# First block of a three-block network: table products as one operation for both parts on VectorE, chunk states stored segment-innermost, one recurrence over all groups

## The chip, the core and the metric

The kernel runs on one core of a Trainium2 chip. Its engines are PE (TensorE, matmuls), DVE (VectorE), ACT (ScalarE), POOL (GpSimd) and SP (SyncE, which here only issues DMAs). Each engine works through its own queue in order and waits on semaphores of the others. The metric is the time of one execution in microseconds (us) on the device; lower is better.

## What is computed

The program runs a first block on 512 tokens of width 1024 and then two layers of another network on its result. The change touches the first block alone, and in it the state-space part (S5). Cut to what matters:

```python
h = rms_norm(x, pre_norm_g);  z = h @ w_in
z_q, z_kv, z_kr, g_attn, u_ssm, g_ssm = split(z)
attn = mla_attention(z_q, z_kv, z_kr, ...)          # 4 heads, 512 tokens
attn = rms_norm(attn) * silu(g_attn)
# S5: 32 groups of 16 channels, 64 complex states each, both directions
lam_bar = exp(lam * dt);  b_bar = (lam_bar - 1) / lam * b
h_t = lam_bar * h_(t-1) + b_bar u_t                  # forward, and reversed
y_t = real(C h_t), summed over the directions, + d_skip * u_t
ssm = gelu(y);  ssm = ssm * sigmoid(ssm @ w_glu + b_glu)
ssm = rms_norm(ssm) * silu(g_ssm)
x = x + rms_norm([attn, ssm] @ w_out)
```

## The kernel before

The 128 partitions hold 64 states of the forward direction and 64 of the reversed one. The 512 tokens are 64 chunks of 8. The 32 groups are worked in 8 slices of 4 groups. For each slice there are three steps, and between the first and the second a recurrence:

- `f_slice(s)`: a table of powers of `lam_bar` times `b_bar` (tiles `tb`, `ot`; factors `FP`, `bbr`, `bbi`), transposed on PE (`ftr`, copied by ACT to `f`) and multiplied with the tokens `U` (`vps`). ACT copies the result into the chunk states `st` (L469, L470).
- `recur(hf)`, once for groups 0 to 15 and once for 16 to 31: DVE carries the state over the 64 chunks. `step` is four DVE operations (L488 to L491: tiles `rt`, `rw`). Seven steps run inside segments of 8 chunks, for all 8 segments at once; six steps carry the segment ends; then the corrections `fx` (L510) are added to `st` (L511).
- `prep(s)`: a table of powers times C (factors `EP`, `cc`), written to DRAM (`Ed`, one DMA for each part), and a short convolution kernel from it (`kps` on PE, `kst` on ACT, three small DVE operations), written to DRAM (`Kd`).
- `y_slice(s)`: reads `Ed` back (tile `e`), reads `Kd` as the matrix `T` in 8 DMAs, copies the states to `X` on ACT, and computes `yps` = U T + X e on PE.

A table is complex, so it has a real and an imaginary part, and each part is two products and a sum: three operations of 128x512. In `f_slice` the real part is computed by DVE and the imaginary by POOL; in `prep` both by POOL (L413, L414, L415, called from `half`).

Around this lie the other parts of the block in the order of the program: the two gate projections (`feat`, 8 feature tiles of 24 matmuls each; ACT `th` and `gate`, DVE `gate` L608), the projection of `z_q`, `z_kv`, `z_kr` (`z_tile`), and the attention heads (`head`, scores in tile `sc`), which run in rounds together with the `y_slice` steps. Weights arrive in 512 KB DMAs into a two-buffer stage `wst`; ACT casts them to `whi` (L136) and DVE computes the rest `wlo` (L137); a product is then three matmuls (L167 to L169).

The order in each engine's queue is not the order of the code: the tile framework's scheduler decides it when the program is built. Tiles share slots by tag (`SLOTS1`); a tile waits for its slot's last reader. `E` has 4 slots of 128x512 for the two parts of two tables.

```python
rounds((s, f_slice(s)) for s in range(8))
for hf in range(2): recur(hf)
# gate projections
for s in range(8): prep(s)
# z projection, V, q
rounds([(HEAD0[h], head(h)) for h in range(4)] + [(SL0 + s, y_slice(s)) for s in range(8)])
```

Of the kernel before, what the change touches and what calls it, by code (L numbers as in the profile page):

```python
# [21 lines left out]
SLOTS1 = {"S": 6, "PT": 4, "E": 4, "et": 1, "X": 2, "K": 1, "T": 2, "Y": 1, "sq": 3, "c": 2, "PW": 1, "U": 1, "C": 1, "w": 4}  # L22
# [41 lines left out]
class Net:  # L64
# [116 lines left out]
    def gain(self, name, l, mark=None, tag="PT"):  # L181
        g = [self.act(name="gain", tag=tag) for _ in range(2)]
# [47 lines left out]
    def load_tile(self, src, t, mark=None, tag="S"):  # L230
        x = [self.act(name="x", tag=tag) for _ in range(2)]
# [66 lines left out]
    def block1(self):  # L298
# [3 lines left out]
        G = 32  # L302
# [114 lines left out]
        br, bi = (sm1([128, G, 16], n) for n in ("bbr", "bbi"))  # L417
# [5 lines left out]
        half(bi, nc.gpsimd, wrb, braw[1], wib, braw[0], OP.add, [128, G, 16], "S")  # L423

        EP, FP = sm1([128, 2, 8, G], "EP"), self.act(shape=[128, 2, 8, G], name="FP", tag="S")
        for r in range(2):
            nc.vector.tensor_copy(FP[0:64, r], PW[0:64, r, 1:9][:, ::-1])
            nc.vector.tensor_copy(FP[64:128, r], PW[64:128, r, 1:9])
# [3 lines left out]
        nc.vector.tensor_copy(EP[0:64, 0], PW[0:64, 0, 0:8])  # L432
        nc.vector.tensor_copy(EP[64:128, 0], PW[64:128, 0, 0:8][:, ::-1])
        nc.vector.tensor_scalar(EP[0:64, 1], PW[0:64, 1, 0:8], -1.0, None, OP.mult)
        nc.vector.tensor_scalar(EP[64:128, 1], PW[64:128, 1, 0:8][:, ::-1], -1.0, None, OP.mult)

        def table(P, xr, xi, s, tags, neg, eng):


            sh = [128, 4, 8, 16]  # L440
            gs = slice(s * 4, s * 4 + 4)
            o = [self.act(shape=sh, name="tb", tag=tags[0]) for _ in range(2)]
            pr, pi = (P[:, r, :, gs].rearrange("p e g -> p g e")[:, :, :, None].to_broadcast(sh) for r in range(2))
            xr, xi = (x[:, :, None, :].to_broadcast(sh) for x in (xr, xi))
# [5 lines left out]
        st = self.act(shape=[128, 2, G, 64], name="st", tag="C")  # L450
        nc.vector.memset(st[:, :, :, 0:1], 0.0)

        def f_slice(s):
            gs = slice(s * 4, s * 4 + 4)
            ft = table(FP, br[:, gs], bi[:, gs], s, ("E", "S"), False, nc.vector)
            yield
            f = []
            for r in range(2):
                p = self.ps("sc" if s % 2 else "tr", "ftr")
                for gg in range(4):  # L460
                    nc.tensor.transpose(p[:, gg * 128:(gg + 1) * 128], ft[r][:, gg], self.ident)
# [3 lines left out]
            pv = self.ps("o", "vps").rearrange("p (r g c) -> p r g c", r=2, g=4)  # L465
            for r in range(2):
                for gg in range(4):
                    mm(pv[:, r, gg], f[r][:, gg], U[:, s * 4 + gg], start=True, stop=True)
            nc.scalar.copy(st[0:64, :, gs, 1:64], pv[0:64, :, :, 0:63])  # L469
            nc.scalar.copy(st[64:128, :, gs, 1:64], pv[64:128, :, :, 63:0:-1])  # L470
# [9 lines left out]
        HG = 16  # L480

        def step(gs, dst, src, e, i, n):

            sh = [128, 2, HG, n]
            t, w = (self.small([128, 2, HG, 8], bufs=1, name=x)[:, :, :, :n] for x in ("rt", "rw"))
            ar = PA[:, 0:1, e, gs].to_broadcast([128, 2, HG])[:, :, :, None].to_broadcast(sh)
            ai = PS[:, i, :, gs][:, :, :, None].to_broadcast(sh)
            nc.vector.tensor_tensor(t, ar, st[:, :, gs, src], OP.mult)  # L488
            nc.vector.tensor_tensor(w, ai, st[:, ::-1, gs, src], OP.mult)
# [3 lines left out]
        def recur(hf):  # L493
            gs = slice(hf * HG, hf * HG + HG)
            for j in range(1, 8):
                n = 8 if j < 7 else 7
                step(gs, slice(1 + j, 64, 8), slice(j, 64 if j < 7 else 56, 8), 0, 0, n)
            for q in range(1, 7):
                step(gs, slice(8 * q + 8, 8 * q + 9), slice(8 * q, 8 * q + 1), 7, 1, 1)
            sh = [128, 8, 7, 7]  # L500
            for gh in range(2):
                g8 = slice(hf * HG + gh * 8, hf * HG + gh * 8 + 8)
                for r in range(2):
                    e = nc.vector
                    d = st[:, r, g8, 8:64].rearrange("p g (s j) -> p g s j", j=8)[:, :, :, 1:8]
                    for r2 in range(2):
                        c = st[:, r2, g8, 8:64:8][:, :, :, None].to_broadcast(sh)
                        pw = PA[:, r ^ r2, 0:7, g8].rearrange("p j g -> p g j")[:, :, None, :].to_broadcast(sh)
                        t = self.act(shape=sh, name="fx", tag="S")
                        e.tensor_tensor(t, c, pw, OP.mult)  # L510
                        e.tensor_tensor(d, d, t, OP.subtract if (r, r2) == (0, 1) else OP.add)  # L511
# [7 lines left out]
        Ed = self.dpool.tile([8, 2, 128, 512], F32, name="Ed")  # L519
        Kd = self.dpool.tile([8, 4, 16, 15, 16], F32, name="Kd").rearrange("s g h j x -> s h g (j x)")  # L520

        def prep(s):
# [69 lines left out]
        for hf in range(2):  # L592
            recur(hf)
# [29 lines left out]
        def z_tile(t):  # L623
# [17 lines left out]
            for i in range(2):  # L641
                nc.gpsimd.tensor_tensor(zn[:, 384 + i * 64:448 + i * 64], ka, kb, OP.add)
# [874 lines left out]
```

## Time and profile before

| | us |
|---|---|
| median of 3 runs (1711.34 to 1712.43) | 1712.42 |
| the profiled execution, its own time | 1714.23 |
| span of that execution, first to last instruction | 1712.4 |

| engine | busy us | share of the span |
|---|---|---|
| PE | 1600.2 | 93% |
| DVE | 1026.3 | 60% |
| ACT | 788.3 | 46% |
| POOL | 502.2 | 29% |

The shares are means over a long program of unlike stages. The first block takes the first 400 us or so of the span, and the rest belongs to the two layers behind it. An engine's share says nothing on a stage: each stage is read with the busy times of that stretch alone. Times given as "start" count from the start of the span.

### The profile page before, as it was taken

The page shows a single profiled execution, that of the slowest core. Times are in us where ns is not written, and L with a number is a line of the kernel's source. Part 1 is how long each engine was busy: PE and PEld are TensorE (multiplying, and loading weights), DVE is VectorE, ACT ScalarE, POOL GpSimd, SP SyncE. Part 2 cuts the span into 40 slices and gives each one's busy share as a digit, 9 for nine tenths or more (in the row PEclk, how much of TensorE's full clock was granted, in tenths as well). Part 3 has the DMA queues.
Part 4 walks back from the last instruction along what each step waited for, and adds up shares of the span by engine and source line. Part 5 has one row for each costly group of instructions (what it writes and reads, how often), then busy time and mean ns, then how long its engine had stood idle before and what let it go on. Part 6 is the DMA issues. An engine that isn't in the chain of part 4 may idle for free.

```text
span 1712.4 us, 22709 instructions
## 1 busy us (share of the span) xinstructions
PE 1600.2 (93%) x8240; PEld 1344.7 (79%) x8240; DVE 1026.3 (60%) x2003; ACT 788.3 (46%) x1540; POOL 502.2 (29%) x557
## 2 busy tenths in 40 slices
PE   7776699989999999999999999999999999999998
PEld 5655588778887878888888888787877888888886
DVE  7999955774589886423333346569986632333334
ACT  5432256743467774333232334358774443314142
POOL 3756622240445551201010122135462110101012
PEclk9888899999999999999999999999999999999999
DMA  4122241353410123233333333430123233332332
GB/s 154 50 68 69 77 133 50 99 195 114 155 32 27 51 80 124 93 99 99 99 99 99 98 99 122 137 101 27 39 70 122 70 99 98 99 98 88 99 96 87
DMA packets 68591, 159.04 MB, mean 93 GB/s; under 512 B 13696, under 2 KB 22400, under 8 KB 68480
## 3 DMA queue, kind: packets, MB, share of 16 engines
q1 hardware_dynamic: 67712, 156.81, 28.9%
q8 instruction: 65, 1.06, 0.3%
q10 hardware_dynamic: 768, 0.79, 0.2%
q14 instruction: 46, 0.38, 0.1%
HBM read 145.80 MB, written 10.98 MB: 92 GB/s over the span
## 4 chain that ended last, share of the span: by engine, by line
PE 71%; DVE 15%; issue 4%; ACT 4%; POOL 3%; DMA 1%; SPq 0%; ACTq 0%; POOLq 0%; DVEq 0%
PE mm L167 20%; PE mm L169 19%; PE mm L168 19%; PE ptr L933 2%; PE cps L973 2%; DVE sc L908 2%; DVE pt L137 1%; DVE wlo L137 1%; PE sc L904 1%; PE oacc L943 1%; PE sc L907 1%; PE oacc L942 1%; ACT ysq L199 1%; POOL rs_r L194 1%; DVE rt L488 1%
## 5 line engine op out<-in xcount | busy, mean ns | idle before, releaser
L137 DVE TENSOR_TENSOR wlo<-wst,whi 128x1024 fp32r<-128x1024 f32 (+3 forms) x209 | 254.9, 1224 | 250.1 <-ACT whi L136 246.4
L136 ACT CAST whi<-wst 128x1024 fp32r<-128x1024 f32 (+3 forms) x209 | 215.2, 1034 | 291.1 <-PE mm L169 125.9
L167 PE MATMUL mm<-xT,whi 128*128 128x512 f32 (+1 forms) x896 | 339.4, 382 | 4.1 <-ACT kf L1073 2.8
L169 PE MATMUL mm<-xT,wlo 128*128 128x512 f32 (+1 forms) x896 | 328.1, 378 | 14.8 <-DVE wlo L137 14.8
L168 PE MATMUL mm<-xT,whi 128*128 128x512 f32 (+1 forms) x896 | 336.6, 377 | 0.0
L1357 POOL TENSOR_TENSOR relu<-relu 128x512 f32<-128x512 f32 x64 | 67.0, 1046 | 539.4 <-ACT relu L1356 539.4
L169 PEld LDWEIGHTS mm<-xT,wlo 128*128 128x128 f32 x896 | 169.6, 190 | 47.7 <-DVE wlo L137 17.5
L169 PE MATMUL mm<-whi,hl 128*128 128x512 f32 x512 | 195.9, 389 | 0.0
L168 PE MATMUL mm<-wlo,hh 128*128 128x512 f32 x512 | 195.9, 389 | 0.0
L167 PEld LDWEIGHTS mm<-xT,whi 128*128 128x128 f32 x896 | 169.1, 190 | 33.7 <-ACT kf L1073 3.6
L168 PEld LDWEIGHTS mm<-xT,whi 128*128 128x128 f32 x896 | 169.8, 190 | 27.8
L167 PE MATMUL mm<-whi,hh 128*128 128x512 f32 x512 | 188.2, 389 | 0.0
L911 ACT ACTIVATE sc<-sc,mn 128x512 f32<-128x512 f32 x192 | 107.3, 560 | 40.1 <-DVE mn L908 36.8
L137 DVE TENSOR_TENSOR hl<-relu,hh 128x512 fp32r<-128x512 f32 x64 | 51.8, 810 | 119.5 <-ACT hh L136 117.3
L137 DVE TENSOR_TENSOR pt<-ptr,pt 128x256 fp32r<-128x256 f32 (+1 forms) x160 | 95.8, 606 | 31.9 <-ACT pt L136 30.4
L169 PEld LDWEIGHTS mm<-whi,hl 128*128 128x128 f32 x512 | 96.1, 188 | 19.9
L167 PEld LDWEIGHTS mm<-whi,hh 128*128 128x128 f32 x512 | 96.1, 188 | 19.9
L168 PEld LDWEIGHTS mm<-wlo,hh 128*128 128x128 f32 x512 | 96.1, 188 | 19.9
L920 POOL TENSOR_SCALAR sc<-sc,smx,gt 128x512 f32<-128x512 f32 (+3 forms) x128 | 80.9, 642 | 92.7 <-DVE smx L915 72.6
L1356 ACT ACTIVATE relu<-mm 128x512 f32<-128x512 f32 x64 | 38.4, 600 | 148.4 <-PE mm L169 148.4
L908 DVE CUSTOM_DVE_ANT_0 sc<-sc,c_mask 128x512 f32<-128x512 f32 x192 | 87.8, 484 | 22.3 <-PE sc L907 20.3
L136 ACT CAST pt<-ptr 128x256 fp32r<-128x256 f32 (+1 forms) x160 | 81.3, 517 | 40.0 <-PE ptr L933 36.3
(406 smaller groups left out, 3131.4 us busy)
## 6 DMA issues: line engine op xcount, KB each, us to landing
wst<-in_w_up_t SPq DMA_DIRECT2D x64, 512.0 KB
wst<-in_w_down_t SPq DMA_DIRECT2D x64, 512.0 KB
wst<-in_w_in_m SPq DMA_DIRECT2D x24, 512.0 KB
wst<-in_w_in_a SPq DMA_DIRECT2D x16, 512.0 KB
x<-x SPq DMA_DIRECT2D x32, 256.0 KB
w<-in_cw SPq DMA_DIRECT2D x32, 256.0 KB
wst<-in_w_out_t SPq DMA_DIRECT2D x16, 512.0 KB
wst<-in_w_in SPq DMA_DIRECT2D x8, 512.0 KB
```

Source lines behind the costliest of these rows:

```text
L136: self.nc.scalar.copy(hi, src)
L137: self.nc.vector.tensor_tensor(lo, src, hi.bitcast(F32), OP.subtract)
L167: mm(ps, lh, rh, start=first, stop=False)
L168: mm(ps, lh, rl, start=False, stop=False)
L169: mm(ps, ll, rh, start=False, stop=last)
L908: nc.vector.tensor_tensor_reduce(out=sreg[i], in0=p, in1=self.mask[:, 512 - w:512], scale=1.0, scalar=3e38, op0=OP.add, op1=OP.min, accum_ ...
L911: self.mark = nc.scalar.activation(sreg[i], sreg[i], AF.Exp, bias=mn[:, i:i + 1], scale=-1.0, accum_out=sm[:, i:i + 1])
L920: nc.gpsimd.tensor_scalar(sreg[i], sreg[i], sm[:, i:i + 1], rgate[:, i:i + 1], OP.mult, OP.mult)
L933: self.pe = nc.tensor.transpose(p[:, c:c + 128], sreg[i][:, j * 128:(j + 1) * 128], self.ident)
L973: nc.tensor.matmul(p[:, :62], st[:, j], bk[:, jj].rearrange("p g n -> p (g n)"), start=jj == 0, stop=jj == 15)
L1356: nc.scalar.activation(a, p, AF.Relu)
L1357: nc.gpsimd.tensor_tensor(a, a, a, OP.mult)
```

## The change

What it does:

- **Tables.** `half` for `bbi` moves from POOL to DVE. `table` makes both parts in one operation on `[128, 4, 16, 16]` (real and imaginary as the upper half of a 16-long axis): three DVE operations of 128x1024 in place of six of 128x512. For this the factors come in pairs, `FP`/`FQ` and `EP`/`EQ`, the second with the parts exchanged and signed; ACT makes all of these but `FP`. POOL has no table operation left.
- **States.** `st` is laid out `[128, G, 2, 8, 8]` with the segment innermost, so that the 8 segments a step works on are 8 adjacent words; before they were 8 words apart. The ACT copies into `st` and out to `X` carry the reordering. `X` becomes two fixed tiles with zeroed edges in place of the zero column of `st`.
- **Recurrence.** One `recur()` over all 32 groups: half as many operations, each of twice the size.
- **Rest.** `Ed` is one DMA of 512 KB for each slice, and so is its read; the `bb` copies go from DVE to ACT, two for each slice in place of four; the two small `zn` additions of a token tile go from POOL to one on DVE. `E` becomes 2 slots of `[128, 2, 512]`.

```diff
-SLOTS1 = {"S": 6, "PT": 4, "E": 4, "et": 1, "X": 2, "K": 1, "T": 2, "Y": 1, "sq": 3, "c": 2, "PW": 1, "U": 1, "C": 1, "w": 4}
+SLOTS1 = {"S": 6, "PT": 4, "E": 2, "et": 1, "K": 1, "T": 2, "Y": 1, "sq": 3, "c": 2, "PW": 1, "U": 1, "C": 1, "w": 4}
...
-        half(bi, nc.gpsimd, wrb, braw[1], wib, braw[0], OP.add, [128, G, 16], "S")
+        half(bi, nc.vector, wrb, braw[1], wib, braw[0], OP.add, [128, G, 16], "S")
...
+        EP, EQ, FP, FQ = (self.act(shape=[128, G, 2, 8], name=n, tag=t)
+                          for n, t in (("EP", "sq"), ("EQ", "sq"), ("FP", "T"), ("FQ", "T")))
+        pw = PW.rearrange("p r e g -> p g r e")
+        nc.vector.tensor_copy(FP[0:64], pw[0:64, :, :, 1:9][:, :, :, ::-1])
+        nc.vector.tensor_copy(FP[64:128], pw[64:128, :, :, 1:9])
+        nc.scalar.activation(FQ[:, :, 0], FP[:, :, 1], AF.Copy, scale=-1.0)
+        nc.scalar.copy(FQ[:, :, 1], FP[:, :, 0])
...
-            half(o[0], eng, pr, xr, pi, xi, OP.add if neg else OP.subtract, sh, tags[1])
-            half(o[1], nc.gpsimd, pi, xr, pr, xi, OP.subtract if neg else OP.add, sh, tags[1])
-            return [t.rearrange("p g e h -> p g (e h)") for t in o]
+            sh = [128, 4, 16, 16]
+            o, t = (self.act(shape=sh, name=n, tag=g) for n, g in (("tb", "E"), ("ot", "et")))
+            for d, p, x in ((o, P, xr), (t, Q, xi)):
+                p = p[:, s * 4:s * 4 + 4].rearrange("p g r e -> p g (r e)")[:, :, :, None].to_broadcast(sh)
+                nc.vector.tensor_tensor(d, p, x[:, :, None, :].to_broadcast(sh), OP.mult)
+            nc.vector.tensor_tensor(o, o, t, OP.add)
+            return o.rearrange("p g (r e) h -> p g r (e h)", r=2)
...
-            nc.scalar.copy(st[0:64, :, gs, 1:64], pv[0:64, :, :, 0:63])
-            nc.scalar.copy(st[64:128, :, gs, 1:64], pv[64:128, :, :, 63:0:-1])
+            for ps_, o in ((slice(0, 64), 1), (slice(64, 128), -1)):
+                nc.scalar.copy(st[ps_, gs].rearrange("p g r j s -> p (g r) j s"),
+                               pv[ps_, :, :, ::o].rearrange("p g r (s j) -> p (g r) j s", j=8))
...
+        def step(dst, src, e, i, n):
+
+            sh = [128, G, 2, n]
+            t, w = (self.act(shape=[128, G, 2, 8], name=x, tag="S")[:, :, :, :n] for x in ("rt", "rw"))
+            ar = PA[:, 0, e, :, None, None].to_broadcast(sh)
+            ai = PS[:, i].rearrange("p r g -> p g r")[:, :, :, None].to_broadcast(sh)
+            nc.vector.tensor_tensor(t, ar, src, OP.mult)
+            nc.vector.tensor_tensor(w, ai, src[:, :, ::-1], OP.mult)
             nc.vector.tensor_tensor(t, t, w, OP.add)
-            nc.vector.tensor_tensor(st[:, :, gs, dst], st[:, :, gs, dst], t, OP.add)
+            nc.vector.tensor_tensor(dst, dst, t, OP.add)
...
+        def recur():
             for j in range(1, 8):
-                n = 8 if j < 7 else 7
-                step(gs, slice(1 + j, 64, 8), slice(j, 64 if j < 7 else 56, 8), 0, 0, n)
+                step(st[:, :, :, j], st[:, :, :, j - 1], 0, 0, 8)
             for q in range(1, 7):
-                step(gs, slice(8 * q + 8, 8 * q + 9), slice(8 * q, 8 * q + 1), 7, 1, 1)
-            sh = [128, 8, 7, 7]
+                step(st[:, :, :, 7, q:q + 1], st[:, :, :, 7, q - 1:q], 7, 1, 1)
+            sh = [128, 16, 7, 7]
...
-            er, ei = table(EP, c_[:, 0], c_[:, 1], s, ("E", "et"), True, nc.gpsimd)
-            for i, e in enumerate((er, ei)):
-                nc.sync.dma_start(Ed[s, i], e.rearrange("p g e -> p (g e)"))
+            e = table(EP, EQ, c_[:, 0], c_[:, 1], s)
+            nc.sync.dma_start(Ed[s], e.rearrange("p g r e -> p (g r e)"))
...
-        for hf in range(2):
-            recur(hf)
+        recur()
```

The built orders differ with it. From the end of the heads on, all queues stand as before. The first place is DVE where the recurrence begins. Before (`rt`, `rw` the first two operations of a step):

```order
L413 TENSOR_TENSOR tb<-FP,bbr 128x512
L415 TENSOR_TENSOR tb<-tb,ot 128x512
L488 TENSOR_TENSOR rt<-PA,st 128x256
L489 TENSOR_TENSOR rw<-PS,st 128x256
L490 TENSOR_TENSOR rt<-rt,rw 128x256
L491 TENSOR_TENSOR st<-st,rt 128x2x128
```

And now:

```order
L456 TENSOR_TENSOR tb<-EP,cc 128x1024
L457 TENSOR_TENSOR tb<-tb,ot 128x1024
L456 TENSOR_TENSOR tb<-EP,cc 128x1024
L616 SCALAR_TENSOR_TENSOR gate<-th,gate 128x512 x2
L498 TENSOR_TENSOR rt<-PA,st 128x512
L499 TENSOR_TENSOR rw<-PS,st 128x512
L500 TENSOR_TENSOR rt<-rt,rw 128x512
L501 TENSOR_TENSOR st<-st,rt 128x64x8
```

Two products of `prep` (`EP`, `cc`) and six of the eight `gate` operations now stand ahead of the recurrence, and its first step spans all groups. The second place is PE behind the z projection: `kps` of `prep` and `ztr`, the transposes of the z tiles. Before:

```order
L539 MATMUL kps<-tb,bb_847 48x128 x7
L646 MATMUL ztr<-c_ident,zn 128x128 x3
L539 MATMUL kps<-tb,bb_848 48x128
```

And now (`zh`, `zl` the normed projection as the moving operand of the last head projections):

```order
L174 MATMUL mm<-zh,whi 128x512
L175 MATMUL mm<-zl,whi 128x512
L176 MATMUL mm<-zh,wlo 128x512
L548 MATMUL kps<-tb,bb_807 48x128 x8
L548 MATMUL kps<-tb,bb_808 48x128 x8
L548 MATMUL kps<-tb,bb_807 48x128 x8
L548 MATMUL kps<-tb,bb_808 48x128 x8
L548 MATMUL kps<-tb,bb_807 48x128 x8
L581 MATMUL yps<-T,U 64x128
L548 MATMUL kps<-tb,bb_808 48x128 x8
```

Before, the 64 `kps` matmuls were spread between other products; now they stand in one run behind all projections, with nothing of the heads' scores ahead of its end.

## Rows read from the trace of the kernel before

**Rows 1.** Busy time by stretch: us, count, TensorE clock, DMA share, GB/s.

```profile
core 0: us, PE busy (x) PEld busy (x) DVE busy (x) ACT busy (x) POOL busy (x), PEclk, DMA share, GB/s
40.00:89.00 49.00, 35.02 (x226) 29.29 (x225) 48.65 (x65) 20.62 (x35) 34.72 (x25) 0.90 0.15 44
89.00:165.00 76.00, 49.51 (x248) 39.65 (x247) 72.91 (x101) 22.98 (x37) 47.58 (x29) 0.84 0.20 58
165.00:214.00 49.00, 34.05 (x159) 27.17 (x157) 48.10 (x109) 11.40 (x31) 28.74 (x25) 0.85 0.32 96
...
242.00:305.00 63.00, 63.00 (x415) 53.29 (x414) 38.69 (x85) 40.80 (x82) 13.65 (x18) 1.00 0.17 46
```

**Rows 2.** Waits of DVE, 40 to 214: waiter, releaser, us, times, longest.

```profile
DVE wlo L137 <- ACT whi L136: 1.8, 1, 1.8
```

**Rows 3.** Waits of PE, 40 to 215, same columns.

```profile
PE mm L169 <- DVE wlo L137: 13.8, 5, 10.9
```

**Rows 4.** Timeline of DVE, table stage: start, us, instruction.

```profile
76.92 0.68 DVE L414 TENSOR_TENSOR ot<-FP,bbi 128x512 f32<-128x512 f32 x1
...
83.19 1.59 DVE L413 TENSOR_TENSOR tb<-FP,bbr 128x512 f32<-128x512 f32 x1
```

**Rows 5.** Timeline of POOL, in brackets the idle time before.

```profile
77.51 1.68 POOL L413 TENSOR_TENSOR tb<-FP,bbr 128x512 f32<-128x512 f32 x1 [3.88 <-PE ftr L461]
...
82.68 1.56 POOL L414 TENSOR_TENSOR ot<-FP,bbi 128x512 f32<-128x512 f32 x1
84.20 1.55 POOL L413 TENSOR_TENSOR tb<-FP,bbr 128x512 f32<-128x512 f32 x1
...
221.11 1.27 POOL L415 TENSOR_TENSOR tb<-tb,ot 128x512 f32<-128x512 f32 x1
```

**Rows 6.** Timeline of DVE while POOL does nothing.

```profile
110.14 0.62 DVE L488 TENSOR_TENSOR rt<-PA,st 128x256 f32<-128x256 f32 x1
...
111.33 0.42 DVE L490 TENSOR_TENSOR rt<-rt,rw 128x256 f32<-128x256 f32 x1
111.79 0.62 DVE L491 TENSOR_TENSOR st<-st,rt 128x256 f32<-128x256 f32 x1
112.44 0.62 DVE L488 TENSOR_TENSOR rt<-PA,st 128x256 f32<-128x256 f32 x1
...
122.00 1.22 DVE L137 TENSOR_TENSOR wlo<-wst,whi 128x1024 fp32r<-128x1024 f32 x1 [1.80 <-ACT whi L136]
123.14 0.21 DVE L488 TENSOR_TENSOR rt<-PA,st 128x32 f32<-128x32 f32 x1
...
127.32 0.22 DVE L488 TENSOR_TENSOR rt<-PA,st 128x32 f32<-128x32 f32 x1
...
128.22 0.22 DVE L488 TENSOR_TENSOR rt<-PA,st 128x32 f32<-128x32 f32 x1
...
129.56 4.71 DVE L510 TENSOR_TENSOR fx<-st,PA 128x392 f32<-128x392 f32 x6
...
134.77 1.52 DVE L511 TENSOR_TENSOR st<-st,fx 128x392 f32<-128x392 f32 x3
```

**Rows 7.** Timeline of PE.

```profile
40.33 0.39 PE L167 MATMUL mm<-xT,whi 128*128 128x512 f32 x1
...
98.06 2.79 PE L468 MATMUL vps<-U,f 128*128 128x64 f32 x24
...
104.19 0.39 PE L167 MATMUL mm<-xT,whi 128*128 128x512 f32 x1
104.41 0.39 PE L168 MATMUL mm<-xT,whi 128*128 128x512 f32 x1
...
242.02 0.63 PE L167 MATMUL sc<-qkh 128*128 128x512 f32 x2
```

**Rows 8.** Chain that ended last: a 512 KB weight load.

```profile
115.68 5.17 DMA wst<-in_w_in
```

**Rows 9.** Timeline of ACT: a copy that writes eight words apart.

```profile
314.45 1.16 ACT L692 ACTIVATE sq<-gth 128x512 f32<-128x512 f32 x1
```

More of the change, by code (lines that the diff above doesn't have):

```diff
@@ L99, in act, with pair @@
         return self.apool.tile(shape or [128, 512], dt, tag=tag, bufs=self.slots[tag], name=name)
+    def pair(self, name, tag):
+        if tag == "E":
+            t = self.act(shape=[128, 2, 512], name=name, tag=tag)
+            return [t[:, 0], t[:, 1]]
+        return [self.act(name=name, tag=tag) for _ in range(2)]
     def fill(self):
@@ L181, in gain @@
     def gain(self, name, l, mark=None, tag="PT"):
-        g = [self.act(name="gain", tag=tag) for _ in range(2)]
+        g = self.pair("gain", tag)
         for i in range(2):
@@ L230, in load_tile @@
     def load_tile(self, src, t, mark=None, tag="S"):
-        x = [self.act(name="x", tag=tag) for _ in range(2)]
+        x = self.pair("x", tag)
         for i in range(2):
@@ L415, in half @@
             e.tensor_tensor(out, out, t, op)
-        br, bi = (sm1([128, G, 16], n) for n in ("bbr", "bbi"))
+        bB = sm1([128, 2, G, 16], "bbar")
+        br, bi = bB[:, 0], bB[:, 1]
         braw = [self.act(shape=[128, G, 16], name="braw", tag="S") for _ in range(2)]
@@ L431, in block1 @@
         nc.vector.tensor_copy(PA[:, :, 0], PW[:, :, 8])
[L432 to L444, printed above, removed]
-            half(o[0], eng, pr, xr, pi, xi, OP.add if neg else OP.subtract, sh, tags[1])
-            half(o[1], nc.gpsimd, pi, xr, pr, xi, OP.subtract if neg else OP.add, sh, tags[1])
-            return [t.rearrange("p g e h -> p g (e h)") for t in o]
@@ L450, in block1, with table @@
-        st = self.act(shape=[128, 2, G, 64], name="st", tag="C")
-        nc.vector.memset(st[:, :, :, 0:1], 0.0)
+        for ps_, o in ((slice(0, 64), 1), (slice(64, 128), -1)):
+            nc.scalar.copy(EP[ps_, :, 0], pw[ps_, :, 0, 0:8][:, :, ::o])
+            nc.scalar.activation(EP[ps_, :, 1], pw[ps_, :, 1, 0:8][:, :, ::o], AF.Copy, scale=-1.0)
+        nc.scalar.copy(EQ[:, :, 0], EP[:, :, 1])
+        nc.scalar.activation(EQ[:, :, 1], EP[:, :, 0], AF.Copy, scale=-1.0)
+        def table(P, Q, xr, xi, s):
+            sh = [128, 4, 16, 16]
[5 more added lines that the diff above has]
+            return o.rearrange("p g (r e) h -> p g r (e h)", r=2)
@@ L453, in f_slice @@
+        st = self.act(shape=[128, G, 2, 8, 8], name="st", tag="C")
         def f_slice(s):
             gs = slice(s * 4, s * 4 + 4)
-            ft = table(FP, br[:, gs], bi[:, gs], s, ("E", "S"), False, nc.vector)
+            ft = table(FP, FQ, br[:, gs], bi[:, gs], s)
             yield
@@ L460, in f_slice @@
                 for gg in range(4):
[L461 removed]
+                    nc.tensor.transpose(p[:, gg * 128:(gg + 1) * 128], ft[:, gg, r], self.ident)
                 f.append(self.act(shape=[128, 4, 128], name="f", tag="PT"))
@@ L464, in f_slice @@
             yield
-            pv = self.ps("o", "vps").rearrange("p (r g c) -> p r g c", r=2, g=4)
+            pv = self.ps("o", "vps").rearrange("p (g r c) -> p g r c", r=2, g=4)
             for r in range(2):
                 for gg in range(4):
-                    mm(pv[:, r, gg], f[r][:, gg], U[:, s * 4 + gg], start=True, stop=True)
-            nc.scalar.copy(st[0:64, :, gs, 1:64], pv[0:64, :, :, 0:63])
-            nc.scalar.copy(st[64:128, :, gs, 1:64], pv[64:128, :, :, 63:0:-1])
+                    mm(pv[:, gg, r], f[r][:, gg], U[:, s * 4 + gg], start=True, stop=True)
+            for ps_, o in ((slice(0, 64), 1), (slice(64, 128), -1)):
+                nc.scalar.copy(st[ps_, gs].rearrange("p g r j s -> p (g r) j s"),
+                               pv[ps_, :, :, ::o].rearrange("p g r (s j) -> p (g r) j s", j=8))
         rounds((s, f_slice(s)) for s in range(8))
@@ L479, in block1 @@
             nc.vector.tensor_copy(PS[:, i, 1], PA[:, 1, e])
[L480 to L489, printed above, removed]
+        def step(dst, src, e, i, n):
[5 more added lines that the diff above has]
+            nc.vector.tensor_tensor(w, ai, src[:, :, ::-1], OP.mult)
@@ L506, in recur @@
                     for r2 in range(2):
[L507 to L511, printed above, removed]
+                        c = st[:, gs, r2, 7:8, 0:7].to_broadcast(sh)
@@ L514, in block1 @@
+                        pw = PA[:, r ^ r2, 0:7, gs].rearrange("p j g -> p g j")[:, :, :, None].to_broadcast(sh)
+                        t = self.act(shape=sh, name="fx", tag="et")
+                        nc.vector.tensor_tensor(t, c, pw, OP.mult)
+                        nc.vector.tensor_tensor(d, d, t, OP.subtract if (r, r2) == (0, 1) else OP.add)
         Dd = sm1([16, G], "Dd")
@@ L518, in block1 @@
             nc.gpsimd.memset(bb, 0.0)
-        Ed = self.dpool.tile([8, 2, 128, 512], F32, name="Ed")
+        Xs = [sm1([128, 4, 2, 66], f"X{i}") for i in range(2)]
+        for X in Xs:
+            nc.gpsimd.memset(X, 0.0)
+        Ed = self.dpool.tile([8, 128, 1024], F32, name="Ed")
         Kd = self.dpool.tile([8, 4, 16, 15, 16], F32, name="Kd").rearrange("s g h j x -> s h g (j x)")
@@ L533, in prep @@
                 ps_, cs_ = slice(d * 64, d * 64 + 64), slice(d * 32, d * 32 + 16)
-                nc.vector.tensor_copy(bb[ps_, 0, :, cs_], br[ps_, gs])
-                nc.vector.tensor_copy(bb[ps_, 1, :, cs_], bi[ps_, gs])
+                nc.scalar.copy(bb[ps_, :, :, cs_], bB[ps_, :, gs])
             p = self.ps("sc", "kps")
             for gg in range(4):
-                for r, e in enumerate((er, ei)):
-                    mm(p[:48, gg * 128:(gg + 1) * 128], bb[:, r, gg], e[:, gg], start=r == 0, stop=r == 1)
+                for r in range(2):
+                    mm(p[:48, gg * 128:(gg + 1) * 128], bb[:, r, gg], e[:, gg, r], start=r == 0, stop=r == 1)
             kst = self.act(shape=[128, 4, 8, 16], name="kst", tag="K")
@@ L556, in y_slice @@
         def y_slice(s):
-            er, ei = (self.act(shape=[128, 4, 128], name="e2", tag="E") for _ in range(2))
-            for i, e in enumerate((er, ei)):
-                nc.sync.dma_start(e.rearrange("p g e -> p (g e)"), Ed[s, i])
+            e = self.act(shape=[128, 4, 2, 128], name="e2", tag="E")
+            nc.sync.dma_start(e.rearrange("p g r e -> p (g r e)"), Ed[s])
             kd = Kd[s]
@@ L564, in y_slice @@
             gs = slice(s * 4, s * 4 + 4)
-            X = self.act(shape=[128, 2, 4, 64], name="X", tag="X")
-            nc.scalar.copy(X[0:64], st[0:64, :, gs])
-            nc.scalar.copy(X[64:128], st[64:128, :, gs, ::-1])
+            X = Xs[s % 2]
+            xv, sv = X.rearrange("p g r c -> p (g r) c"), st[:, gs].rearrange("p g r j s -> p (g r) s j")
+            nc.scalar.copy(xv[0:64, :, 2:66].rearrange("p a (s j) -> p a s j", j=8), sv[0:64])
+            nc.scalar.copy(xv[64:128, :, 0:64][:, :, ::-1].rearrange("p a (s j) -> p a s j", j=8), sv[64:128])
             yield
@@ L572, in y_slice @@
                 mm(p[0:64, c], U[:, s * 4 + gg], T[:, gg], start=True, stop=False)
-                mm(p[0:64, c], X[:, 0, gg], er[:, gg], start=False, stop=False)
-                mm(p[0:64, c], X[:, 1, gg], ei[:, gg], start=False, stop=True)
+                mm(p[0:64, c], X[:, gg, 0, 1:65], e[:, gg, 0], start=False, stop=False)
+                mm(p[0:64, c], X[:, gg, 1, 1:65], e[:, gg, 1], start=False, stop=True)
             if s % 2 == 0:
@@ L640, in z_tile @@
                                     rS[:, t].rearrange("p (a f) -> p a f", a=2), OP.mult)
-            for i in range(2):
-                nc.gpsimd.tensor_tensor(zn[:, 384 + i * 64:448 + i * 64], ka, kb, OP.add)
+            nc.vector.tensor_tensor(zn[:, 384:512].rearrange("p (i f) -> p i f", i=2),
+                                    *(a[:, None, :].to_broadcast([128, 2, 64]) for a in (ka, kb)), OP.add)
             yield
```

11 lines of the change are left out of this document (2 added, 9 removed).

## Prediction

> **What bounds the kernel now.** I first read the busy times by stretch [rows 1]. Outside the first block PE is the limit; from 242 to 305 us, when heads and `y_slice` run, it is busy for 63.0 of 63 us at full clock. From 40 to 214 us it is not: PE works 35.0 of 49, 49.5 of 76 and 34.1 of 49 us, at 0.84 to 0.90 of its clock, and DVE is busy 48.7, 72.9 and 48.1 us of the same stretches. The waits agree: in those 174 us DVE waits 1.8 us in all [rows 2], while PE's longest wait, 10.9 us, is for a `wlo` of DVE [rows 3]. So before 214 us the DVE queue sets the time, and what leaves it counts.
>
> Much of that busy time is not work. The same product of 128x512 takes 0.68 us at 76.92 and 1.59 us at 83.19 [rows 4]. At the first POOL was idle (3.88 us before 77.51); at the second it was between two table operations of its own, 1.56 and 1.55 us [rows 5]. DVE and POOL take turns. POOL's last table operation begins at 221.11 [rows 5], so a chain DVE-POOL carries the front of the block to about 222 us.
>
> **Prices.** Alone, DVE runs 1024 contiguous elements in 1.14 us from start to start (122.00 to 123.14), 1.04 ns an element and some 0.07 fixed [rows 6]; so 512 are 0.60. A `step` operation on words 8 apart is dearer: 256 elements take 0.62 us where the contiguous addition takes 0.42 [rows 6], about 1.8 ns an element. A step of four dependent operations is 2.30 us from 110.14 to 112.44, a serial one 0.90 (127.32 to 128.22), `fx` 0.78 each (4.71 for 6, 2.0 ns an element, a factor read at a stride), `st` in L511 0.5 each, at the contiguous rate though in runs of 7 [rows 6]. PE begins a 512-column matmul every 0.22 to 0.23 us and a small one every 0.11 to 0.12 (2.79 for 24) [rows 7]; I use 0.23 and 0.11, the latter for all small ones, an estimate.
>
> **The sum, stage by stage.** I walk the new order of the queues with these prices.
>
> *Tables.* On DVE, from the first product at about 43 us (what lies ahead of it hardly changes) to the recurrence: 24 table operations and two early ones of `prep` at 1.14 (29.6), six `wlo` (6.8), six gates at 0.60 (3.6), the small powers some 3: 43 us, to 86. POOL is gone, so all are at the lone price. But the recurrence over all groups needs the last slice, and its `vps` stands late on PE: from 40.33 [rows 7] PE has 144 matmuls at 0.23 (33.1), 128 records of `vps`, 64 `ftr` and 32 `utr` at 0.11 (24.6), 57.7 us, and waits about 2 for the third and fourth `wlo`; then ACT makes a gate and copies the states, about 1.5. So the recurrence begins at about 101 and DVE stands idle some 15 us ahead of it, in part behind tables that want a slot of `E`.
>
> *Recurrence.* Seven steps of 512 at 0.60 with 0.11 for each of three dependences (2.75): 19.3. Six serial ones of 64 elements, 32 more in each of four operations at 1.8 ns (0.23): 1.13, 6.8. Sixteen `fx` and sixteen additions of 784 elements, 0.89 each: eight of either, with dependence 1.0: 16. Together 42.1. Before, at the lone prices, both halves cost 14 x 2.30 + 12 x 0.90 + 16 x 0.78 + 16 x 0.5 = 63.5, and more beside POOL. Between them now stand gates, the z weights, z tiles, V and q: 24.5 us at 1.04 ns an element. The z tiles come just behind PE, ACT and POOL, so I add 6 for waits. End: 101 + 42 + 25 + 6 = 174.
>
> *Prep.* 22 operations at 1.14 (25.1), small ones 3, dependences 1.5, less 1 behind the last sum: 28.6, to 202.5. PE does only `kps` here, 14 us of work: it starves, where before it had z and V to do.
>
> *Restart.* The first `y_slice` needs its 512 KB from `Ed`, issued behind the last write; a load of that size took 5.17 us [rows 8]: 207.5. Its 24 records at 0.11 end at 210, and the first score follows. Before, the first score was at 242.02 [rows 7], with two more slices done (48 records, 5.3 us) and nine head matmuls fewer (2.1): a like state at 238.8. The lead is 29 us. I take off 3 for the second slice's load and for PE's lower clock behind idle time (0.84 to 0.90 in the stretches where it idled [rows 1]): 26. From there PE is busy in an unchanged order, so the lead stays to the end.
>
> Edits priced at nothing: `EP`, `EQ`, `FQ` on ACT, some 6 us at 38 to 50 us, under PE's projections; FQ is wanted only behind the first two products. A copy at a stride of eight words takes 1.16 us on ACT for 512 elements [rows 9]; if the `st` and `X` copies do, ACT gains 0.6 x 32, of which 1.2 lies ahead of the recurrence and the rest beside PE; without that cover it would cost up to 10. `Ed` in one DMA of twice the size: the next but one table waits for it, about 4 us of DVE work later, and I count it hidden; at the 5.17 us it would cost 1 for each of six slices, the low half of which is in the range. The `zn` additions on DVE are 0.2 each, in the 24.5.
>
> The sum is made against the profiled execution, 1714.2 (span 1712.4 and 1.8 around it): 1688. The median lies 1.8 below that execution, so the forecast is **1686**.
>
> **Where rows leave two prices.** A `step` operation now reads and writes runs of 8 words, 64 words apart. The trace has a contiguous price (1.04 ns) and a strided one (1.8 to 2.0), and none for this. At the strided one three of four operations cost 0.41 more in seven steps (8.6), and eight `fx` 0.7 more (5.4): 14 us, a gain of 12, 1700. I take the contiguous one, since L511 ran at it in runs of 7 [rows 6].
> The Trainium skill (Vector Engine (DVE) Microarchitecture Reference, 5.2 Measured stream behaviour on trn2) says that a port streams at full rate when its elements come in runs of at least two adjacent words from an 8-byte boundary, whatever the hop between. No run here shows runs of eight; by that rule the sum stays at 1686, by the strided rows it is 1700.
>
> **Rivals.**
> *A late recurrence.* One recurrence waits for all slices, where the first half waited for four. If PE runs its 58 us at the 0.90 of the clock that this stretch had [rows 1], everything behind is 6 us later: 1692. For it: PE still waits for `wlo`. Against: PE has less to wait for now.
> The Trainium skill (Perfetto Trace Analysis, Optimizing Scalar/DVE Operations) gives the same warning: where DVE is not saturated but makes others wait, smaller instructions may finish sooner. By it this rival, 1692, is the outcome.
> *The strided price*, 1700, above.
> *Fewer waits.* If the z waits (6), PE's 2 and the take-off of 3 vanish, the gain is 37: 1675. Against: DVE waits on three engines in turn there.
> *Slower.* Tables broadcast both operands in four dimensions at 1024 elements. If these ran at the 2.0 ns of `fx`, each costs 1.0 more: 22 us in prep, and 26 in the tables, of which 11 are hidden behind PE. 37 us against a gain of 26: 1723. It decides from about 1.8 us an operation. Against it: the old products have the same broadcasts and ran 512 in 0.68 us [rows 4].
> *No change.* The diff removes POOL's tables in the built order, so this needs a new wait of 26 us, such as SP's queue: it issues some 46 DMAs between the `prep` tables in order, and each read of `Kd` blocks it until the write has landed.
>
> **How the numbers follow.** Forecast case (1679 to 1690) 0.45; fewer waits (below 1679) 0.17; late recurrence (1690 to 1696) 0.14; strided price (1696 to 1706) 0.14; no change to within 0.2%, about what a measurement of this kernel can tell, 0.04; slower 0.06. The range for 8 in 10 reaches over all the faster cases: 1671 to 1702. Faster by over 0.2%: 0.90.
>
> **What would show it.** Right: no table operation on POOL; products of 128x1024 at about 1.2 us; `rt` and `st` of 128x512 near 0.7; the first `rt` near 101 us, after an idle time of DVE with PE or ACT as its end; PE idle beside `kps` from about 150 to 200; the first score near 210. Wrong: `rt` near 1.0 (strided price); products near 2.1 (slower); a first `rt` beyond 107 (late recurrence); DVE waiting for `Ed` or `Kd` in `prep`, or PE waiting for `e` and `T` behind the first score, which would eat the lead.

## Result, and the profile after

The kernel after takes 1686.86 us (median of 4 runs, 1685.29 to 1689.21), the kernel before on the same chip 1712.43: a ratio of 0.985 (95% interval 0.983 to 0.987), 25.6 us faster. The forecast was 1686. The profiled executions are 1714.23 and 1685.29 us.

Busy time by stretch, as in [rows 1]: microseconds, then busy time and count of PE, PEld, DVE, ACT and POOL, PE's clock, DMA share, GB/s.

```profile
40.00:89.00 49.00, 49.00 (x327) 43.46 (x326) 43.50 (x62) 32.51 (x56) 0.00 (x0) 1.00 0.29 84
89.00:165.00 76.00, 60.90 (x279) 49.66 (x278) 63.05 (x125) 31.43 (x60) 4.43 (x8) 0.91 0.16 47
165.00:214.00 49.00, 32.51 (x189) 27.12 (x188) 33.08 (x50) 12.28 (x31) 0.00 (x0) 0.76 0.50 155
```

POOL has left the table stage, and PE, which was busy for 35.0 of the first 49 us, is now busy for all of them at full clock. But DVE, busy for 48.7, 72.9 and 48.1 us before, is so for 43.5, 63.1 and 33.1: it has less to do and also waits. Its timeline (start, duration; in brackets the idle time before, and what ended it) shows the first place, ahead of the recurrence:

```profile
82.18 1.22 DVE L456 TENSOR_TENSOR tb<-EP,cc 128x1024 f32<-128x1024 f32 x1
83.31 1.22 DVE L457 TENSOR_TENSOR tb<-tb,ot 128x1024 f32<-128x1024 f32 x1
89.85 1.23 DVE L456 TENSOR_TENSOR tb<-EP,cc 128x1024 f32<-128x1024 f32 x1 [5.32 <-PE ftr L471]
92.35 0.69 DVE L616 SCALAR_TENSOR_TENSOR gate<-th,gate 128x512 f32<-128x512 f32 x1 [1.27 <-ACT gate L615]
96.31 0.69 DVE L616 SCALAR_TENSOR_TENSOR gate<-th,gate 128x512 f32<-128x512 f32 x1 [3.27 <-ACT gate L615]
98.04 0.69 DVE L498 TENSOR_TENSOR rt<-PA,st 128x512 f32<-128x512 f32 x1 [1.04 <-ACT st L480]
98.65 0.68 DVE L499 TENSOR_TENSOR rw<-PS,st 128x512 f32<-128x512 f32 x1
99.36 0.69 DVE L500 TENSOR_TENSOR rt<-rt,rw 128x512 f32<-128x512 f32 x1
100.09 0.69 DVE L501 TENSOR_TENSOR st<-st,rt 128x512 f32<-128x512 f32 x1
100.82 0.69 DVE L498 TENSOR_TENSOR rt<-PA,st 128x512 f32<-128x512 f32 x1
...
166.88 0.97 DVE L518 TENSOR_TENSOR st<-st,fx 128x784 f32<-128x784 f32 x1
167.89 1.22 DVE L456 TENSOR_TENSOR ot<-EQ,cc 128x1024 f32<-128x1024 f32 x1
169.15 1.22 DVE L457 TENSOR_TENSOR tb<-tb,ot 128x1024 f32<-128x1024 f32 x1
```

DVE stands idle 10.9 us in four pieces between 84.5 and 98.0, while two tables of `prep` have only their first product (82.18 and 89.85). Their second, `ot<-EQ`, comes at 167.89, directly behind the last operation of the recurrence. Nothing in these rows says why; run e5 does. A step is 2.78 us (98.04 to 100.82).

The second place is at the end of the tables. The first block shows DVE, the second ACT, whose `kst` (L551) has one slot:

```profile
197.36 1.21 DVE L457 TENSOR_TENSOR tb<-tb,ot 128x1024 f32<-128x1024 f32 x1
...
202.71 0.21 DVE L557 TENSOR_TENSOR k<-k,dd 16x64 f32<-16x64 f32 x1 [3.88 <-ACT k L553]
...
211.48 0.21 DVE L557 TENSOR_TENSOR k<-k,dd 16x64 f32<-16x64 f32 x1 [4.23 <-ACT k L553]
```

```profile
196.38 0.58 ACT L551 COPY kst<-kps 48x512 f32<-48x512 f32 x1
196.98 0.20 ACT L553 COPY k<-kps 16x64 f32<-16x64 f32 x1
201.88 0.58 ACT L551 COPY kst<-kps 48x512 f32<-48x512 f32 x1 [4.69 <-DMA Kd<-kst]
...
205.82 0.58 ACT L551 COPY kst<-kps 48x512 f32<-48x512 f32 x1 [3.14 <-DMA Kd<-kst]
```

The last table ends at 198.57, but each `kst` waits until the one before it has been written to `Kd`. PE's next `kps` waits for ACT in turn, and the first score follows the last of them:

```profile
202.73 3.26 PE L548 MATMUL kps<-tb,bb 128*48 128x128 f32 x16 [3.11 <-ACT k L553]
205.83 0.38 PE L582 MATMUL yps<-e,X 128*64 128x128 f32 x2
...
208.33 0.50 PE L174 MATMUL sc<-qkh 128*128 128x512 f32 x1
```

### The profile page after: what moved, and what is told of

Its sections match the earlier page's. It is cut to its first block, busy times and chain, and to the rows that moved or that the text cites. A ratio compares the mean times of both kernels' runs of the same rounds, so it can differ in the third digit from the quotient of the medians.

```text
span 1683.5 us, 22526 instructions
## 1 busy us (share of the span) xinstructions
PE 1593.7 (95%) x8240; PEld 1344.8 (80%) x8240; DVE 980.2 (58%) x1927; ACT 804.3 (48%) x1564; POOL 382.1 (23%) x476
## 4 chain that ended last, share of the span: by engine, by line
PE 76%; DVE 11%; ACT 5%; issue 3%; DMA 3%; POOL 2%; SPq 1%; ACTq 0%; DVEq 0%; POOLq 0%
PE mm L174 21%; PE mm L176 21%; PE mm L175 20%; PE ptr L941 2%; DVE sc L916 2%; PE cps L981 2%; DVE pt L144 1%; PE oacc L951 1%; PE sc L912 1%; PE sc L915 1%; PE oacc L950 1%; DVE wlo L144 1%; PE vps L478 1%; ACT ysq L206 1%; DMA w<-in_cw 1%
## 5 line engine op out<-in xcount | busy, mean ns | idle before, releaser
L1364 ACT ACTIVATE relu<-mm 128x512 f32<-128x512 f32 x64 | 38.2, 598 | 148.5 <-PE mm L176 148.5
L143 ACT CAST pt<-ptr 128x256 fp32r<-128x256 f32 (+1 forms) x160 | 81.5, 517 | 39.6 <-PE ptr L941 35.7
```

The costliest lines, as they stand in the source:

```text
L143: self.nc.scalar.copy(hi, src)
L1364: nc.scalar.activation(a, p, AF.Relu)
```

## Experiments

Each kernel was timed beside the kernel before on one chip; I compare ratios to before. "us" behind a ratio is the ratio less 1, times 1712.4. The kernel after is 0.9852, -25.3 us. The intervals reach some 2 to 5 us to either side.

**e1: only the engine.** The kernel before; three words are changed:

```
-        half(bi, nc.gpsimd, ...
+        half(bi, nc.vector, ...
-            half(o[1], nc.gpsimd, ...
+            half(o[1], nc.vector, ...
-            er, ei = table(EP, ..., True, nc.gpsimd)
+            er, ei = table(EP, ..., True, nc.vector)
```

> The kernel before with nothing changed but the engine of the table operations: all 96 of 128x512 on DVE, none on POOL; old layout, two recurrences. Theory 1 (the engines took turns, so POOL's share was never done beside DVE's; the gain of 26 us needs less DVE work too): DVE has 16 x 6 x 0.66 = 63 us of tables, 63.5 of recurrence at lone prices, 38 of the rest, 9 of small copies and 10 of waits, 183 from 40 us on, to 223, where the chain DVE-POOL ended at 222: 1712 within 6. rt of 128x256 falls from 1.08 to about 0.62. Theory 2 (POOL's slow operations are the cause; taking them off is enough): 1690 within 5.

Measured: 0.9777 (0.9761 to 0.9794), -38.2 us. Theory 1 is wrong. Theory 2 is right in its cause, but its 22 us were too few: taking POOL off is enough, and it gives more than the whole change. The rest of the change must then cost, on balance, some 13 us by the ratios (6.6 by the spans of the two profiled executions, 1676.9 and 1683.5). The windows of e1 show DVE nearly without idle time:

```profile
40.00:89.00 49.00, 47.76 (x306) 41.31 (x306) 48.76 (x99) 28.10 (x44) 0.00 (x0) 1.00 0.27 84
89.00:165.00 76.00, 64.55 (x353) 52.88 (x353) 73.42 (x180) 28.22 (x60) 13.93 (x16) 0.93 0.34 108
```

It works 122.2 of 125 us there; in the kernel after it works 106.6. The 183 us of work that I had put down for e1 was too much: DVE is busy 166.6 us from 40 to 214, and the last operation of the recurrence starts at 207.3. As expected, `rt` of 128x256 falls from 1.08 us in the mean to 0.65.

**e2: all but the engine.** The kernel after with the tables split as before:

```
+            for r in range(2):
+                e, h, sr = nc.vector if P is FP and r == 0 else nc.gpsimd, [128, 4, 8, 16], slice(r * 8, r * 8 + 8)
...
-                nc.vector.tensor_tensor(d, p, x[:, :, None, :].to_broadcast(sh), OP.mult)
...
+                    e.tensor_tensor(d[:, :, sr], p, x[:, :, None, :].to_broadcast(h), OP.mult)
```

> The kernel after with the tables as before (real part of the first ones on DVE, all else on POOL, operations of 128x512), but the new layout and the one recurrence. Theory 1: POOL's chain of the last six tables of prep, 6 x 9.4 us (1.9, 1.3, 1.5 twice), starts only when slots come free and sets the end again: 1705 to 1718. Theory 3 (the shorter recurrence alone gives the gain): 1690 within 5.

Measured: 0.9885 (0.9871 to 0.99), -19.7 us, between the two. DVE is busy for 8.8 of the 20 us from 165 to 185, POOL for 19.5: POOL's chain does set the end, at a lower price than I gave it. So either half of the change alone gives 20 or 38 us, and both together 25. What the engine is worth depends on the rest: 38.2 us in the kernel before, 5.7 between e2 and the kernel after.

**e3: real and imaginary part apart, on DVE** (the loop of e2 with `e = nc.vector`).

> The kernel after, all tables on DVE, but real and imaginary part apart: six operations of 128x512 in place of three of 128x1024. By fixed cost (0.07 an operation, 0.11 a dependence) a table takes 4.0 instead of 3.6 us: eight tables of prep stand on the path, +3 us, 1690; the others lie under PE. Rival (prep is not set by DVE's tables but by the chain kps, kst, write of Kd): within 1 us of after, 1687.

Measured: 0.9853 (0.9835 to 0.9871), no difference to after that the intervals show. They would hide the 3 us expected, and in the profiled execution the first score comes at 213.2, 4.9 us later than in the kernel after (208.3). So it stays open what one operation for both parts is worth here; it is no more than a few microseconds.

**e4: two slots for `kst`** (`"K": 1` becomes `"K": 2`).

> The kernel after with two slots for kst instead of one. Theory 4 (in prep ACT's kst waits for the write of the kst before, 15.1 us in six times, and with it the k operations and the next kps): the waits go, the last kps comes 4 to 6 us earlier, 1681 to 1683. Rival (the first score waits for the loads of y_slice or for the last table anyway): within 1 us of after, 1687.

Measured: 0.9781 (0.9766 to 0.9796), -37.5 us, 12 better than after where 4 to 6 were expected. The last `kps` matmul starts at 195.5 in place of 205.7, the first score's `QR` matmul (L725) at 196.5 in place of 209.1. The last table ends at 193.7, so the last `kps` follows it by 1.8 us, where it took 7.1 in the kernel after (198.6 to 205.7). So the chain of `kst`, not the tables, set the restart. Some 3 of the 12 us lie ahead of it: the recurrence ends at 164.8 in place of 167.9, with 2 us less of DVE's waits, and no run shows why.

**e5: `fx` back to slots of its own.** The built order of DVE puts no `ot` of `prep` between the steps of the recurrence. The change had moved `fx` from the six slots of `S` to the tag `et`, in a line that the diff above leaves out; `ot` has that tag too, it has one slot, and `fx` comes first in the program.

```
-            sh = [128, 16, 7, 7]
+            sh = [128, 8, 7, 7]
-            for gh in range(2):
-                gs = slice(gh * 16, gh * 16 + 16)
+            for gh in range(4):
+                gs = slice(gh * 8, gh * 8 + 8)
...
-                        t = self.act(shape=sh, name="fx", tag="et")
+                        t = self.act(shape=sh, name="fx", tag="S")
```

> The kernel after with fx over 8 groups at a time in the slots of S, as before, in place of the one slot of et that the table's second product (ot) also uses; nothing else is changed. Differences are to the kernel before, timed on the same chip (the kernel after stands at -25.5 us). Theory 6 (a table of prep cannot be finished until the last fx has left et, so all of prep stands behind the recurrence, and DVE sits idle 11 us ahead of it and some 10 us behind): tables of prep fill the idle time, the first kps comes near 110 us in place of 170, -36 to -46. Theory 5 (the one recurrence waits for the last slice, and that alone is the loss against run e1): -23 to -28, since fx in twice as many operations is 3 us dearer.

Measured: 0.9691 (0.9667 to 0.9715), -52.9 us (1660.31 us median), beyond what theory 6 gave. The idle time ahead of the recurrence fills with tables of `prep`, and their steps then mix (DVE's timeline of e5):

```profile
85.30 1.23 DVE L456 TENSOR_TENSOR ot<-EQ,cc 128x1024 f32<-128x1024 f32 x1
86.56 1.23 DVE L457 TENSOR_TENSOR tb<-tb,ot 128x1024 f32<-128x1024 f32 x1
...
116.58 1.21 DVE L457 TENSOR_TENSOR tb<-tb,ot 128x1024 f32<-128x1024 f32 x1
...
117.98 0.67 DVE L501 TENSOR_TENSOR st<-st,rt 128x512 f32<-128x512 f32 x1
118.58 1.21 DVE L456 TENSOR_TENSOR ot<-EQ,cc 128x1024 f32<-128x1024 f32 x1
```

The first `kps` starts at 108.4 in place of 170.4, the last table ends at 156.4, and the first score's L725 is at 190.5. From 101 to 185 us DVE is busy for 80.75 of 84 us.

**e6: e5 with two slots for `kst`.**

> The kernel of e5 with two slots for kst. Theory 6: with prep spread out, the write of Kd is done before the next kst, and the second slot is worth 2 us or less over e5. Theory 4 (kst's one slot is a loss of its own): at least 8 us better than e5.

Measured: 0.9699 (0.968 to 0.9718), the same as e5 within the intervals, where theory 4 wanted 8 us. With `prep` spread out, the one slot of `kst` costs nothing that these runs can show.

**e7: e5 with two recurrences** (`step` and `recur` take 16 groups, `recur(0)` and `recur(1)`).

> The kernel of e5 with two recurrences of 16 groups in the new layout in place of one. Theory 5 (one recurrence over all groups starts too late): 5 to 11 us better than e5. Rival (DVE has other work to fill the wait with, so only the work counts: two recurrences cost 14 steps of 1.9 and 12 serial ones of 1.1 against 7 of 2.8 and 6 of 1.1, 13 us more, a part of it hidden): equal to e5 or up to 10 us slower.

Measured: 0.9744 (0.9721 to 0.9768), 9.1 us slower than e5. DVE is busy for 30.7 of 31 us from 70 to 101, so the wait is gone, but that time bought nothing, for in e5 only 4.7 us of it are left. Theory 5 falls. The group of the last score matmuls, with its first and last start in us, e5 first:

```profile
L726 PE MATMUL sc<-zl,QR x16: 388/392/401, 190.7 to 243.5; 128*128 128x512 f32 x16
L728 PE MATMUL sc<-zl,QR x16: 388/392/401, 196.5 to 247.9; 128*128 128x512 f32 x16
```

In this pair of executions 4.4 us, about half of the difference, are there when the scores end (247.9 less 243.5); the rest comes in work that the edit does not touch.

**e8: segments outermost.** The states are stored so that a step's operands stand 8 words apart.

```
-        st = self.act(shape=[128, G, 2, 8, 8], name="st", tag="C")
+        st = self.act(shape=[128, G, 2, 8, 8], name="st", tag="C").rearrange("p g r s j -> p g r j s")
```

> The kernel after with the states' last two dimensions exchanged, so that one step's operands stand 8 words apart again as before; the number and size of operations stays. By the strided row of before (0.62 for 256 elements where contiguous ones took 0.42) three of a step's four operations of 512 cost 0.4 more, rt 1.1 instead of 0.69: 8.6 us in seven steps, and X and st copies on ACT get 0.5 cheaper each, where ACT waits: 6 to 12 us slower than after, -14 to -20 against before. Rival (runs of 8 and words 8 apart cost the same, or it is hidden): within 2 us of after.

Measured: 0.9922 (0.99 to 0.9945), 12.0 us slower than after. Groups of DVE's instructions (busy, mean ns, idle before):

```profile
L518 DVE TENSOR_TENSOR st<-st,fx 128x784 f32<-128x784 f32 x8 | 12.7, 1592 | 0.1
L517 DVE TENSOR_TENSOR fx<-st,PA 128x784 f32<-128x784 f32 x8 | 12.7, 1591 | 0.1
...
L498 DVE TENSOR_TENSOR rt<-PA,st 128x512 f32<-128x512 f32 x7 | 7.9, 1122 | 2.4 <-ACT st L480 2.2
...
L500 DVE TENSOR_TENSOR rt<-rt,rw 128x512 f32<-128x512 f32 x7 | 4.9, 693 | 0.1
```

Three of a step's four operations take 1.12 to 1.16 us in the mean, the contiguous sum (L500) still 0.69. In the kernel after all four are 0.69, and `fx` is 0.97.

**e9: the control of e5**, smaller `fx` in the old slot (e5 with the tag `et`).

> Control for e5: fx over 8 groups at a time, as there, but still in the one slot of et. Differences are to the kernel before on the same chip (after -25.5, e5 -53.5). Theory 6 (what counts is the slot, not the size): the tables of prep stay behind the recurrence, twice as many fx operations cost up to 3 us, -21 to -26. Rival (smaller fx operations free the slot sooner and let other work in, so size is the cause): -36 or better.

Measured: 0.984 (0.9813 to 0.9867), -27.4 us, that of after within the intervals. The first `kps` is at 171.1. It is the slot.

**e10: e5 with real and imaginary part apart.**

> The kernel of e5 with real and imaginary part of a table apart, six operations of 512 in place of three of 1024. From 101 to 185 us DVE is busy in e5 for 80.8 of 84 us, so its work is on the path: 6 x 0.62 against 3 x 1.14 is 0.3 us for each of 8 to 14 tables there, 2 to 5 us slower than e5, -48 to -52. Rival (one operation for both parts is worth nothing here either, as in e3): within 1.5 us of e5.

Measured: 0.9704 (0.969 to 0.9719), 2.2 us slower than e5. The intervals overlap, so this stays open; it is no more than a few microseconds.

**e11: e5 with the tables of `prep` on POOL.**

> The kernel of e5 with the eight tables of prep on POOL (48 operations of 128x512); the first eight stay on DVE. Theory 1 (DVE and POOL take turns): DVE loses 29 us of work of its own, but what stands beside POOL's 48 operations at 1.3 to 1.9 us (75 us) gets 1.6 to 2 times as long, and POOL's chain ends later: -15 to -35, that is 18 to 38 us slower than e5. Rival (POOL's work is done beside DVE's): DVE, the bound from 101 to 185 us, is 29 us lighter, -55 to -75.

Measured: 0.9781 (0.9763 to 0.9799), 15.4 us slower than e5, just under the range of theory 1, far from the rival. Its tables are in two halves, as in e10, and against e10, from which it differs in the engine alone, it is 13.2 us slower. The first block shows DVE, the second POOL, which waits from 102.34 to 110.23:

```profile
104.26 0.68 DVE L501 TENSOR_TENSOR rw<-PS,st 128x512 f32<-128x512 f32 x1
...
113.66 1.78 DVE L500 TENSOR_TENSOR rt<-PA,st 128x512 f32<-128x512 f32 x1
115.36 1.54 DVE L501 TENSOR_TENSOR rw<-PS,st 128x512 f32<-128x512 f32 x1
```

```profile
110.23 2.95 POOL L458 TENSOR_TENSOR tb<-EP,cc 128x512 f32<-128x512 f32 x2 [7.89 <-PE kps L550]
113.15 1.74 POOL L459 TENSOR_TENSOR tb<-tb,ot 128x512 f32<-128x512 f32 x1
```

The same `rw` takes 0.68 us while POOL is idle and 1.54 while it works.
The Trainium skill (SBUF — State Buffer, Who interferes with whom) says that a DVE instruction with two SBUF inputs contends with a GpSimd instruction that reads SBUF. These rows and [rows 4, 5] agree.

## Why the forecast came out, and where its steps failed

- *Contention* was the right cause. A product took 0.68 or 1.59 us before [rows 4]; products of 128x1024 now take 1.22 throughout, and e1 and e11 show the price of POOL from both sides: -38.2 us for taking it off, 13.2 (against e10) for giving back 48 of its 72 operations. Not all of it is contention, though. In e2, POOL needs 1.03 us for a product even while DVE stands idle, from 177.5 to 187.7, where DVE needed 0.68:

```profile
181.91 2.07 POOL L458 TENSOR_TENSOR ot<-EQ,cc 128x512 f32<-128x512 f32 x2
```

  How the 38.2 us divide between the two was not separated.
- *The new layout* was priced rightly: a step at 2.78 us (2.75 put down). The strided price, the rival at 1700, did not come; e8 shows that it would have been real, 12 us where I gave 14. Taking the runs of 8 for contiguous was right. The last two lines of [rows 6], which gave the prices of `fx` and L511, run past 131.71, where POOL starts again; in e1, where POOL makes no table, six `fx` take 4.50 us in place of 4.71, so the price hardly moves (in [rows 6] it was POOL that gave way: its two products from 131.71 on took 10.20 us).
The Trainium skill (Vector Engine (DVE) Microarchitecture Reference, 5.2 Measured stream behaviour on trn2) has full rate for runs of two adjacent words or more that start on an 8-byte boundary: 0.69 us for 512 in runs of 8, and 1.12 in e8, where no two words of the states are adjacent, agree.
- *Tables*: the recurrence began at 98.0 (101 put down) and ended at 167.9 (174), *prep*'s tables took 30.7 us (28.6) and ended at 198.6 (202.5). From the first to the last operation the recurrence took 69.9 us (73). The waits in it were 5.5 us (6) and the other work 24.7 (24.5); what was put too high is the recurrence itself, 39.6 us (42.1), above all its serial steps, 5.5 (6.8), and `fx` with its additions, 15.1 (16, for eight of either and not sixteen).
- *Restart* is the step that failed in its mechanism. I let the first `y_slice` wait for its 512 KB (207.5); the first score was to come at 210 and came at 208.3. But what PE waited for was `kps`, held by the one slot of `kst` (e4): from the last table to the first score it took 9.8 us, where the sum has 7.5 for another reason. The term came near by chance.
- *The idle time ahead of the recurrence* was foreseen (15 us; 10.9 measured), but I put it down to PE's late slices and tables waiting for `E`, and took `prep` behind the recurrence as given. It was an effect of the change: `fx` moved from `S` to the one slot of `et`. That move alone costs 25.5 us, between e5 and e9, which differ in the slot only. I costed operations and durations and not the slots that a tag shares.
- *A late recurrence*, as a rival, did not come: PE ran at a clock of 1.00 from 40 to 89 us, not at 0.90, and the first `rt` came 3 us early. With other work to fill the wait, one recurrence beats two by 9.1 us (e7); in the kernel after itself, where nothing fills it, two were not run.
The Trainium skill (Perfetto Trace Analysis, Optimizing Scalar/DVE Operations) advises smaller instructions where DVE is not saturated but holds others up. In e5 DVE is busy for 80.75 of 84 us, so the condition is not met there, and the split did not pay. The same page (Identifying Performance Opportunities, Optimization Strategy) says that consistent bubbles can mean too little room for the next tile. The six waits of `kst` for its one slot, which e4 takes away, agree; the idle time that e5 fills is no such repeated gap.
- *Slower* and *fewer waits* did not occur: the broadcast products ran at 1.22 us, and the waits came. (In *slower*, the 11 us hidden behind PE do not follow from the 15 us of idle time that the sum gives DVE there.)
- *The lead* was 30.5 us at the first score, by the same conversion (238.8 less 208.3), and is 26.5 at the last score, the kernel before first:

```profile
L718 PE MATMUL sc<-zl,QR x16: 392/397/400, 243.2 to 294.8; 128*128 128x512 f32 x16
L726 PE MATMUL sc<-zl,QR x16: 388/394/399, 209.4 to 268.3; 128*128 128x512 f32 x16
```

  So 4 us were lost where I took off 3. At the end of the spans it is 28.9. The difference arises behind the heads, in work that the change does not touch, where PE was granted a lower clock in the kernel before (the same stretch of work, columns as in [rows 1], before first):

```profile
364.90:410.70 45.80, 40.96 (x217) 34.96 (x216) 27.53 (x48) 19.08 (x42) 9.94 (x14) 0.93 0.38 115
338.20:381.20 43.00, 38.18 (x218) 32.95 (x217) 27.48 (x47) 18.91 (x41) 9.86 (x14) 1.00 0.41 122
```

  The medians differ by 25.6, near the 26 of the sum.

In sum, the engine is worth 38.2 us (e1), the other edits together another 14.7 (e5 against e1), and the shared slot, with `fx` in larger pieces, takes 27.6 back (e5 to after). My 26 was the right total of parts that I had partly wrong, and some luck: an earlier start and a shorter recurrence (6.1 us together) stand against longer tables and a longer restart (4.3). How the 14.7 divide stays open: two recurrences cost 9.1 and the strides 12.0, but in different surroundings, and ACT's `X` copies became dearer (1.16 in place of 0.62 us, while the `st` copies stayed at 0.58), which no run took apart. The best version is e5, 1660.31 us, with e6 its equal.

## What to carry to other kernels

When a change moves a tile to another tag, list the tiles that wait for the same slot and which of them the program allocates first; one slot shared by two stages puts them one behind the other, and no duration shows it. Moving two-input work from GpSimd to VectorE can pay although VectorE then has more of its own to do (e1), since here each slowed what the other did. When a change gives the forecast total, test its parts alone all the same: here one part alone beat the whole.

## What the runs showed of the hardware

- `fx`, 784 elements with a broadcast operand, takes 0.97 us in the new layout and 1.59 in e8, where the states' words stand 8 apart. In pieces of 392 it takes 0.55 in e5 and 0.78 before [rows 6]. It has a broadcast operand in all of them, so the stride set the price.
- ACT pays for a stride in SBUF, whether it reads or writes it: `X` copies of 64x512, which read the states, take 1.16 us in the kernel after and 0.62 in e8; `st` copies, which write them, take 0.58 and 1.14. In the kernel after the `st` copies read PSUM at a stride of eight words, and that costs them nothing (before, without it, they took 0.57 for 504 elements).
- A small operation suffers most beside POOL: in e11 `rt` of 128x64 takes 0.81 us in the mean, and 0.28 in e8, where POOL computes no table. In e2 three operations of 16x64 take 1.18, 0.98 and 1.08 us beside POOL's products of 1.03, and one takes 0.21 at 177.11, when POOL stands idle. That fits a wait for a whole operation of POOL, which no run shows by itself.
- The stretch behind the heads that is shown above, from the first `mm<-whi,xT` there to the first `mm<-xT,whi`, is the same work in every run. It takes 43.0 to 43.1 us where PE is granted full clock (after, e1, e2, e8, e11), 44.4 to 44.7 at 0.96 (e3, e5, e9, e10) and 45.8 to 45.9 at 0.93 (before, e4, e7). So up to 2.9 us between two runs need not come from the edit.
